# A hybrid encoder trunk: values of mixer C on 128 columns, squares of mixer A in PSUM, another order of the first transposes

## The chip, the cores and the metric

The kernel runs on one core of a Trainium2 chip. The metric is the time of one execution in device microseconds (us). The engines: PE (TensorE, products and transposes, writes PSUM), ACT (ScalarE), DVE (VectorE), POOL (GpSimd) and SP (here only a queue that issues DMAs). PSUM has eight banks of 128 partitions x 512 fp32 numbers.

## What is computed

256 tokens x 1024 channels in float32 go through two layers:

```
h = RMSNorm(x);  q,k,v of four mixers and four gates = split(h @ W_in)      # W_in: 1024 x 12544
A: differential attention, 4 heads of 128:  o = RMSNorm((softmax(q0 k0) - lam softmax(q1 k1)) v)
B: grouped-query attention, 8 heads       D: 2-D neighbourhood attention, 8 heads
C: dilated attention, 8 heads of 64: three groups of keys, (window, dilation) = (128,1), (512,4), (2048,16);
   the groups' outputs are combined by their softmax denominators
x += (sum_i sigmoid(gate_i) * (o_i @ P_i)) @ W_out
x += (silu(a) * b) @ W_down,   [a|b] = DWConv3(RMSNorm(x) @ W_up)           # 1024 x 5632, 2816 x 1024
```

For mixer C with 256 tokens, one softmax over the keys of all three groups gives the combination. A query sees up to 256 keys of group 0, and of groups 1 and 2 only keys of its own residue class. The kernel orders the tokens so that the first and the last 64 partitions of a tile of 128 queries belong to two classes with 64 keys each.

## The kernel before

**Weights.** The work is a list of jobs, 56 for the mixers of a layer and then W_out, W_up and W_down. A job is one load of 1 MB of weights (tile `w`, three buffers, on SP's queue, three jobs ahead), two splits of it and its products. A split (`split`) makes a high part on ACT (line 281) and the rest on DVE (line 282). A product of fp32 accuracy is three matmuls of such parts (`mm3`, lines 334 to 336): high by high, high by rest, rest by high. A block of the first projection (512 columns, 256 tokens) takes two jobs of 24 matmuls each and two PSUM banks of the tag `mm`, which has four; the other tags are `s` (one bank, scores), `tp` (two, transposes), `o` (one, products with values). Blocks come in the order of a string, `... gD1 vC0 qC0 qC2 bD1 kC2 vC1 vC2 gB0 ...`: q, k, v of a mixer and group, g a gate, b a branch product.

**Behind a block.** `qk_vec` normalises and rotates a block of q or k: squares on ACT into the tile `sq` (line 468), rotation on DVE (lines 479 and 480, which read the `mm` bank), a reduction of `sq` (line 482), rsqrt on POOL. `sq` has one buffer, which `sumsq` (the norms) and mixer A's `finish` take as well. A block of values is copied by ACT (lines 811, 817).

**Mixers.** A unit is one step of a mixer for 128 queries: `score` (scores, maximum, exponential), 1.25 jobs later `transp`, 2 jobs after the scores `pv`, the product with the values into `o`. `finish` divides by the denominators when the last unit of a tile is done. C has 8 units (heads) for each of 2 tiles, 0.8 jobs apart; A has 4 units for each tile.

**The order.** The program is traced job by job: after each quarter of a job's matmuls the functions hung there (`at`) are traced. From this a planner that simulates the engines fixes, when the kernel is built, the order of instructions on every engine and which instruction gets a buffer; earlier traced ones go first when they are ready. `behind(i)` keeps what is traced in it behind instruction `i` on `i`'s engine. On the chip every engine runs its list in order and waits at semaphores.

**The start** (`first_norm`). x comes by SP's and ACT's queues, the first weights in parts. PE runs products on zeros, spreads the row of gains over 128 partitions (line 1174), and transposes the normed x (line 420) in four sets (tile 0 or 1, half 0 or 1 of the channels), each evacuated by ACT (line 434) and DVE (line 437) into `hTh` and `hTl`. The first job's matmuls start on set (0, 0).

Of the kernel before, what the change touches and what calls it, by code (L numbers as in the profile page):

```python
# [10 lines left out]
F32 = mybir.dt.float32  # L11
F32R = mybir.dt.float32r
AF = mybir.ActivationFunctionType
ALU = mybir.AluOpType
AX = mybir.AxisListType

DM = 1024
# [9 lines left out]
MA, MB, MC, MD = range(4)  # L27
# [59 lines left out]
class Trunk:  # L87
# [324 lines left out]
            scaled(i)  # L412
        return xn

    def norm_tr(self, t, xn, by_token=False, halves=(0, 1)):

        for i in halves:
            p = self.ps("mm")
            for k in range(4):
                self.last_tr = self.nc.tensor.transpose(p[:, k * 128:(k + 1) * 128], xn[:, i * 512 + k * 128:i * 512 + (k + 1) * 128], self.ident).ins  # L420
            hl = [a[:, i * 4:i * 4 + 4, :] for a in (self.hTh, self.hTl)]
            if not by_token:
                last = self.evac_split([(four(p), *(half(a, t) for a in hl))])
                continue
            pv = p.rearrange("p (k u c r) -> p u k c r", k=4, u=2, c=16)
            tv = [a.rearrange("p k (r c u) -> p u k c r", r=4, c=16) for a in hl]
            last = self.evac_split([(pv[:, u], tv[0][:, 2 * t + u], tv[1][:, 2 * t + u]) for u in range(2)])
        return last
# [193 lines left out]
    def pv(self, u):  # L622
        nc = self.nc
        if u["m"] == MA and u["k"] % 2 == 0:
            return
        m, t, st, pt = u["m"], u["t"], u["st"], u["pt"]
        o = st.setdefault("o", {})
        if t not in o:
            o[t] = self.ps("o")
        o = o[t]  # L630
        v = st["v"]
        blk = lambda i: pt[:, i * 128:(i + 1) * 128]
        if m == MC:
            h = u["h"]
            s = slice(h * 64, (h + 1) * 64)
            for i in range(2):
                nc.tensor.matmul(o[:, s], blk(i), v[0][:, i, s], start=i == 0, stop=False)  # L637
            for b in range(2):
                nc.tensor.matmul(o[64 * b:64 * b + 64, s], blk(2)[:, 64 * b:64 * b + 64], v[1 + b][:, t, s], start=False, stop=True)
        elif m == MD:  # L640
            for i in range(4):
                h = 2 * i + u["k"]
                hs = slice(h * 64, (h + 1) * 64)
                for s in range(2):
                    nc.tensor.matmul(o[64 * s:64 * s + 64, hs], blk(i)[:, 64 * s:64 * s + 64], v[1 + t][:, s, hs], start=True, stop=True)
        elif m == MA:
            for c in range(2):
                h = u["k"] - 1 + c
                s = slice(h * 128, (h + 1) * 128)
                for i in range(2):  # L650
                    nc.tensor.matmul(o[:, s], blk(2 * c + i), v[0][:, i, s], start=i == 0, stop=i == 1)
        else:

            g, par = u["k"] // 2, u["k"] % 2
            ph, pl = (a.rearrange("p (i k q) -> p k i q", i=2, k=2) for a in pt)
            for i in range(2):
                vh, vl = (v[:, j, i, g * 64:g * 64 + 64] for j in range(2))
                self.mm3(o[:64, par * 256:(par + 1) * 256], ph[:, i], pl[:, i], vh, vl, i == 0, i == 1, stationary_w=True)
            if par:
                self.o_over_q(st, o, slice(2 * g, 2 * g + 2), t * 128, 128)  # L660
                del st["o"][t]
            return
        if u["last"]:
            self.finish(u, o)

    def finish(self, u, o):

        nc = self.nc
        m, t, st = u["m"], u["t"], u["st"]
        sums = st["sums"][t]  # L670
        nh = 4 if m == MA else 8
        d = 512 // nh
        hv = lambda a: a.rearrange("p (h d) -> p h d", d=d)
        if "osb" not in st:
            st["osb"] = self.t4([128, 2, 512])
        osb = st["osb"]
        r = self.small("rcp", 8)
        if m == MA:

            nc.vector.reciprocal(r[:, :4], sums.rearrange("p (h c) -> p h c", c=2)[:, :, 0])  # L680
            sq = self.sb(self.tp, "sq", [128, 2, 512], F32, bufs=1)[:, 0]
            nc.vector.tensor_tensor(hv(osb[:, t, :]), hv(o[:]), r[:, :4].unsqueeze(2).to_broadcast([128, 4, 128]), ALU.mult)
            nc.scalar.activation(sq, osb[:, t, :], AF.Square, scale=1.0 / math.sqrt(128.0))
            rr = self.small("rr", 4)
            nc.vector.tensor_reduce(rr, hv(sq[:]), AX.X, ALU.add)
            self.rsqrt_mean(rr[:, :4], rr[:, :4], 4)
            nc.vector.tensor_tensor(hv(osb[:, t, :]), hv(osb[:, t, :]), rr.unsqueeze(2).to_broadcast([128, 4, 128]), ALU.mult)
        else:
            nc.vector.reciprocal(r, sums)
            nc.vector.tensor_tensor(hv(osb[:, t, :]), hv(o[:]), r.unsqueeze(2).to_broadcast([128, 8, 64]), ALU.mult)  # L690
# [29 lines left out]
    def layer(self, l):  # L720
        nc = self.nc
# [75 lines left out]
        def vblock(m, col0, g=0):  # L797
# [4 lines left out]
            def ev():  # L802
                v = stt[m]["v"]
                if g == 0:
                    v.append(self.t4([128, 2, 512]))
                elif g == 1:
                    v.extend([self.t4([128, 2, 512]), self.t4([128, 2, 512])])
                for t in range(2):
                    o = cell["o"][t]
                    if g == 0:  # L810
                        nc.scalar.copy(v[0][:, t, :], o)
                        continue

                    for b in range(2):
                        r = slice(64 * b, 64 * b + 64)
                        w = r if g == 1 else slice(64 - 64 * b, 128 - 64 * b)
                        nc.scalar.copy(v[1 + b][w, t, :], o[r])

            def windows():

# [100 lines left out]
        for what in ORDER.split():  # L921
            kind, i, c = what[0], "ABCD".index(what[1]), int(what[2:] or 0)
            if what == "kB":
                bkv()
            elif kind in "qk":
                k = int(kind == "k")
                col0 = ((AQ, BQ, CQ, DQ), (AK, None, CK, DK))[k][i] + c * 512
                first = slot[0] == 0
# [211 lines left out]
    def first_norm(self):  # L1140

        nc, d = self.nc, self.d
        zero = self.sb(self.wp, "hi", [128, 1024], F32R, bufs=5)
        nc.vector.memset(zero[:].bitcast(F32), 0.0)
        warm = self.small("warm", 1, 1)
        nc.scalar.activation(warm, self.mhalf[:, :1], AF.Exp)
        job = self.jobs[0]
        job["w"] = self.sb(self.wp, "w", [128, 2048], F32, bufs=3)
        (dst, src), = job["src"](job["w"][:])
        part = lambda k, n: (dst[:, k:k + n], bass.AP(src.tensor, src.offset + k * 128 * N_IN, [src.ap[0], (src.ap[1][0], n), src.ap[2]]))  # L1150
        xrows = lambda u: (self.x[64 * (u % 2):64 * (u % 2) + 64, u // 2, :], self.rows("x", u, 0, DM))
        row = self.t4([1, DM])

        nc.sync.dma_start(*xrows(0))
        nc.scalar.dma_start(*xrows(1))
        nc.scalar.dma_start(*part(0, 1))
        nc.sync.dma_start(row, self.dram("norm1_g", 0, [[DM, 1], [1, DM]]))
        nc.sync.dma_start(*part(1, 1))
        nc.sync.dma_start(*part(2, 2))
        for u in (2, 3):  # L1160
# [4 lines left out]
        p = self.ps("s")  # L1165
        ones = self.small("ones", 128, 1)[:1]
        nc.gpsimd.memset(ones, 1.0)
        for i in range(10):
            last = nc.tensor.matmul(p, zero[:, :128], zero[:, :512], start=True, stop=True).ins

        g = [self.ps("tp") for i in range(2)]
        with self.behind((last,)):
            for i in range(2):
                nc.tensor.matmul(g[i], ones, row[:, i * 512:(i + 1) * 512], start=True, stop=True)

        def norm(t):
            ss = self.small("ss", 4)
            for i in range(2):
                self.sumsq(t, slice(i * 512, (i + 1) * 512), ss, i, vector=(t, i) == (0, 1))
            return self.norm_vec(t, g, ss, 2, lazy=True)  # L1180


        xn = [norm(0)]
# [1 line left out]
        with self.behind((self.last_xn,)):  # L1185
            self.split(0)
        with self.behind((self.last_split,)):
            last = self.norm_tr(0, xn[0][0], halves=(0,))
        with self.behind(last):
            self.split(1)  # L1190
            xn.append(norm(1))
            xn[1][1](0)

        def step(t, i, then):
            with self.behind((self.last_mm, self.last_split)):
                last = self.norm_tr(t, xn[t][0], halves=(i,))
            with self.behind(last):
                then()

        def first():  # L1200
            xn[0][1](1)
            self.split(2)

        def second():
            xn[1][1](1)
            self.split(3)

        def third():
            self.split(4)
            self.split(5)  # L1210

        self.at(0, 1, lambda: step(1, 0, first))
        self.at(0, 3, lambda: step(0, 1, second))
        self.at(1, 1, lambda: step(1, 1, third))
        self.at(1, 3, lambda: self.split(6))

def trunk_kernel(tc, d):
    with ExitStack() as ctx:
# [29 lines left out]
```

## Time and profile before

| | |
|---|---|
| three timed runs | 1246.92, 1249.25, 1251.32 us; median 1249.25 |
| profiled execution | 1249.13 us, span 1247.3 us, mean granted TensorE clock 0.993 |
| busy: PE, DVE, ACT, POOL | 1223.9, 901.3, 716.8, 134.4 us |

The span runs from the first instruction to the last; the execution's own time is a little longer. "Busy" counts the time in which an engine computes. PE's matmuls overlap in the pipeline, so a matmul's duration is longer than the distance to the next one; where rates matter, the text takes differences of start times.

### The profile page before, as it was taken

The page shows a single profiled execution, that of the slowest core. Times are in us where ns is not written, and L with a number is a line of the kernel's source. Part 1 is how long each engine was busy: PE and PEld are TensorE (multiplying, and loading weights), DVE is VectorE, ACT ScalarE, POOL GpSimd, SP SyncE. Part 2 cuts the span into 40 slices and gives each one's busy share as a digit, 9 for nine tenths or more (in the row PEclk, how much of TensorE's full clock was granted, in tenths as well). Part 3 has the DMA queues.
Part 4 walks back from the last instruction along what each step waited for, and adds up shares of the span by engine and source line. Part 5 has one row for each costly group of instructions (what it writes and reads, how often), then busy time and mean ns, then how long its engine had stood idle before and what let it go on. Part 6 is the DMA issues. An engine that isn't in the chain of part 4 may idle for free.

```text
span 1247.3 us, 18889 instructions
## 1 busy us (share of the span) xinstructions
PE 1223.9 (98%) x7394; PEld 1049.6 (84%) x7394; DVE 901.3 (72%) x1445; ACT 716.8 (57%) x1197; POOL 134.4 (11%) x88
## 2 busy tenths in 40 slices
PE   8999999989999999999999999999899999999998
PEld 5878888877888889998878888888688888999986
DVE  5997787874455679887478978869555456888853
ACT  4556767536444467665355766655455443777641
POOL 0332130320000000000023212203200000000000
PEclk8999999989999999999999999999999999999999
DMA  8757345444346646565544754374434353666551
GB/s 257 231 168 237 106 165 170 147 156 142 129 154 168 202 136 201 194 202 199 201 163 147 215 186 136 114 225 138 166 135 156 116 167 122 203 204 200 183 194 66
DMA packets 127671, 212.09 MB, mean 170 GB/s; under 512 B 9085, under 2 KB 56797, under 8 KB 127582
## 3 DMA queue, kind: packets, MB, share of 16 engines
q1 hardware_dynamic: 125758, 205.64, 50.3%
q0 software_dynamic: 1280, 4.20, 1.6%
q8 instruction: 58, 0.95, 0.3%
q10 hardware_dynamic: 544, 1.05, 0.3%
q14 instruction: 31, 0.25, 0.1%
HBM read 203.53 MB, written 1.05 MB: 164 GB/s over the span
## 4 chain that ended last, share of the span: by engine, by line
PE 95%; DMA 2%; ACT 1%; DVE 1%; issue 0%; ACTq 0%; SPq 0%
PE mm L334 18%; PE mm L336 18%; PE mm L335 18%; PE mm L332 6%; PE mm L331 6%; PE mm L330 6%; PE tp L613 2%; DMA w<-in_w_in_dram 2%; PE tp L334 2%; PE tp L335 2%; PE tp L336 2%; PE tp L493 1%; PE o L637 1%; PE s L532 1%; PE o L334 1%; PE o L335 1%
## 5 line engine op out<-in xcount | busy, mean ns | idle before, releaser
L282 DVE TENSOR_TENSOR lo<-w,hi 128x1024 fp32r<-128x1024 f32 x376 | 456.1, 1221 | 209.0 <-ACT hi L281 207.3
L281 ACT CAST hi<-w 128x1024 fp32r<-128x1024 f32 x376 | 392.4, 1052 | 298.6 <-PE mm L336 184.6
L334 PE MATMUL mm<-hi,hTh 128*128 128x512 f32 (+1 forms) x796 | 314.2, 396 | 11.5 <-DVE qn L480 7.6
L335 PE MATMUL mm<-lo,hTh 128*128 128x512 f32 (+1 forms) x796 | 313.3, 394 | 0.8 <-DVE lo L282 0.8
L336 PE MATMUL mm<-hi,hTl 128*128 128x512 f32 (+1 forms) x796 | 313.3, 395 | 0.0
L330 PE MATMUL mm<-hTh,hi 128*128 128x256 f32 x704 | 193.9, 276 | 1.2 <-ACT hTh L434 1.2
L332 PE MATMUL mm<-hTl,hi 128*128 128x256 f32 x704 | 194.1, 276 | 0.9 <-DVE hTl L437 0.9
L331 PE MATMUL mm<-hTh,lo 128*128 128x256 f32 x704 | 194.1, 276 | 0.0
L334 PEld LDWEIGHTS mm<-hi,hTh 128*128 128x128 f32 x796 | 151.0, 190 | 43.1 <-issue 8.7
L336 PEld LDWEIGHTS mm<-hi,hTl 128*128 128x128 f32 x796 | 150.6, 189 | 30.9 <-DVE hTl L437 1.7
L335 PEld LDWEIGHTS mm<-lo,hTh 128*128 128x128 f32 x796 | 150.8, 190 | 30.4 <-DVE lo L282 1.4
L330 PEld LDWEIGHTS mm<-hTh,hi 128*128 128x128 f32 x704 | 131.9, 188 | 1.7 <-ACT hTh L434 1.7
L332 PEld LDWEIGHTS mm<-hTl,hi 128*128 128x128 f32 x704 | 132.0, 188 | 1.3 <-DVE hTl L437 1.3
L331 PEld LDWEIGHTS mm<-hTh,lo 128*128 128x128 f32 x704 | 132.2, 188 | 0.0
L160 POOL TENSOR_TENSOR sm_qr<-sm_qr,mhalf 128x16 f32<-128x16 f32 (+1 forms) x24 | 81.1, 3380 | 2.0
L334 PE MATMUL mm<-hi,t 128*128 128x512 f32 (+1 forms) x192 | 74.6, 389 | 0.0
L335 PE MATMUL mm<-lo,t 128*128 128x512 f32 (+1 forms) x192 | 73.6, 383 | 0.0
L336 PE MATMUL mm<-hi,t 128*128 128x512 f32 (+1 forms) x192 | 73.0, 384 | 0.0
L1054 ACT ACTIVATE e<-mm,cwT 128x256 f32<-128x256 f32 x88 | 47.0, 560 | 27.8 <-PE mm L332 25.4
L402 POOL TENSOR_TENSOR sm_nr<-sm_nr,mhalf 128x1 f32<-128x1 f32 x8 | 4.4, 550 | 526.7 <-DVE sm_nr L399 517.9
L159 POOL TENSOR_SCALAR sm_qr<-sm_qr 128x16 f32<-128x16 f32 (+1 forms) x24 | 30.6, 1274 | 238.9 <-DVE sm_qr L482 238.7
L1055 DVE SCALAR_TENSOR_TENSOR e<-mm,cwT,e 128x255 f32<-128x255 f32 x88 | 39.6, 478 | 12.0 <-ACT e L1054 12.0
(177 smaller groups left out, 1670.0 us busy)
## 6 DMA issues: line engine op xcount, KB each, us to landing
w<-in_w_in_dram SPq DMA_DIRECT2D x97, 1024.0 KB, 5.1
w<-in_w_up_dram SPq DMA_DIRECT2D x44, 1024.0 KB, 5.1
w<-in_w_down_dram SPq DMA_DIRECT2D x22, 1024.0 KB, 4.9
w<-in_w_branch_dram SPq DMA_DIRECT2D x16, 1024.0 KB, 4.9
w<-in_w_out_dram SPq DMA_DIRECT2D x8, 1024.0 KB, 5.7
t<-t POOLq DMA_DIRECT2D x16, 256.0 KB, 5.6
t<-t SPq DMA_DIRECT2D x32, 64.0 KB, 3.1
t<-in_rpb_dram SPq DMA_DIRECT2D x32, 62.5 KB, 5.2
```

The source lines that it names most:

```text
L159: nc.gpsimd.tensor_scalar(dst, ss, EPS, None, op0=ALU.add)
L160: nc.gpsimd.tensor_tensor(dst, dst, mh, ALU.pow)
L281: self.nc.scalar.copy(hi, w)
L282: self.last_split = self.nc.vector.tensor_tensor(lo, w, hi[:].bitcast(F32), ALU.subtract).ins
L330: mm(out, wh, xh, start=first, stop=False)
L331: mm(out, wl, xh, start=False, stop=False)
L332: mm(out, wh, xl, start=False, stop=last)
L334: mm(out, xh, wh, start=first, stop=False)
L335: mm(out, xh, wl, start=False, stop=False)
L336: self.last_mm = mm(out, xl, wh, start=False, stop=last).ins
L1054: nc.scalar.activation(y[:, b:b + 256], o[:, b:b + 256], AF.Identity, scale=cw(1, z), bias=cw(3, z))
L1055: nc.vector.scalar_tensor_tensor(y[:, b + 1:b + 256], o[:, b:b + 255], cw(0, z), y[:, b + 1:b + 256], op0=ALU.mult, op1=ALU.add)
```

## The change

In C's `pv` the product with the values of group 0 repeats the 64 columns of a head, and groups 1 and 2 of both classes are one product, whose 128 columns are the two classes. Of each query row the half of its own class counts; `finish` takes it from there, after heads 0 to 3 and after heads 4 to 7 of a tile. The value tiles of groups 1 and 2 are laid out by query tile and class instead. A's `finish` writes its squares over its product in PSUM. At the start the row of gains goes by POOL's queue, its spreading comes after four of the products on zeros, the sets of transposes are evacuated from the banks `o` and `s`, and their places change: sets (1, 0) and (0, 1) after the first half of job 0, set (1, 1) after its third quarter.

```diff
-    def norm_tr(self, t, xn, by_token=False, halves=(0, 1)):
+    def norm_tr(self, t, xn, by_token=False, halves=(0, 1), tag="mm"):
-            p = self.ps("mm")
+            p = self.ps(tag)
...
         if m == MC:
+            oh = o[:, h % 4 * 128:h % 4 * 128 + 128]
             for i in range(2):
-                nc.tensor.matmul(o[:, s], blk(i), v[0][:, i, s], start=i == 0, stop=False)
-            for b in range(2):
-                nc.tensor.matmul(o[64 * b:64 * b + 64, s], blk(2)[:, 64 * b:64 * b + 64], v[1 + b][:, t, s], start=False, stop=True)
+                nc.tensor.matmul(oh, blk(i), v[0][:, i, s].unsqueeze(1).to_broadcast([128, 2, 64]), start=i == 0, stop=False)
+            nc.tensor.matmul(oh, blk(2), v[1 + t][:, :, s], start=False, stop=True)
+            if h % 4 == 3:
+                self.finish(u, o)
+                del st["o"][t]
+            return
...
         if m == MA:
-            sq = self.sb(self.tp, "sq", [128, 2, 512], F32, bufs=1)[:, 0]
-            nc.scalar.activation(sq, osb[:, t, :], AF.Square, scale=1.0 / math.sqrt(128.0))
+            nc.scalar.activation(o, osb[:, t, :], AF.Square, scale=1.0 / math.sqrt(128.0))
-            nc.vector.tensor_reduce(rr, hv(sq[:]), AX.X, ALU.add)
+            nc.vector.tensor_reduce(rr, hv(o[:]), AX.X, ALU.add)
+        elif m == MC:
+            h0 = u["h"] - 3
+            nc.vector.reciprocal(r[:, :4], sums[:, h0:h0 + 4])
+            for b in range(2):
+                w = slice(64 * b, 64 * b + 64)
+                nc.vector.tensor_tensor(hv(osb[w, t, h0 * 64:h0 * 64 + 256]), o[w].rearrange("p (h b d) -> p h b d", h=4, b=2)[:, :, b, :],
+                                        r[w, :4].unsqueeze(2).to_broadcast([64, 4, 64]), ALU.mult)
...
-                        nc.scalar.copy(v[1 + b][w, t, :], o[r])
+                        nc.scalar.copy(v[1 + t][w, b, :], o[r])
...
+        row = self.t4([1, DM])
+        nc.gpsimd.dma_start(row, self.dram("norm1_g", 0, [[DM, 1], [1, DM]]))
-        nc.sync.dma_start(row, self.dram("norm1_g", 0, [[DM, 1], [1, DM]]))
...
-        for i in range(10):
-            last = nc.tensor.matmul(p, zero[:, :128], zero[:, :512], start=True, stop=True).ins
-        with self.behind((last,)):
-            for i in range(2):
-                nc.tensor.matmul(g[i], ones, row[:, i * 512:(i + 1) * 512], start=True, stop=True)
+        last = None
+        for i in range(12):
+            with self.behind(last):
+                if i in (4, 5):
+                    last = nc.tensor.matmul(g[i - 4], ones, row[:, (i - 4) * 512:(i - 3) * 512], start=True, stop=True)
+                else:
+                    last = nc.tensor.matmul(p, zero[:, :128], zero[:, :512], start=True, stop=True)
+                last = (last.ins,)
...
-                self.sumsq(t, slice(i * 512, (i + 1) * 512), ss, i, vector=(t, i) == (0, 1))
+                self.sumsq(t, slice(i * 512, (i + 1) * 512), ss, i, vector=i == 1)
...
-            last = self.norm_tr(0, xn[0][0], halves=(0,))
+            last = self.norm_tr(0, xn[0][0], halves=(0,), tag="o")
         with self.behind(last):
             self.split(1)
+            xn[0][1](1)
             xn.append(norm(1))
-            xn[1][1](0)
+            for i in range(2):
+                xn[1][1](i)
...
-        self.at(0, 1, lambda: step(1, 0, first))
-        self.at(0, 3, lambda: step(0, 1, second))
-        self.at(1, 1, lambda: step(1, 1, third))
+        def second():
+            with self.behind((self.last_mm, self.last_xn)):
+                last = self.norm_tr(1, xn[1][0], halves=(0,), tag="s")
+            with self.behind((self.last_tr, *last)):
+                last = self.norm_tr(0, xn[0][0], halves=(1,), tag="o")
+            with self.behind(last):
+                self.split(2)
+        def third():
+            with self.behind((self.last_mm, self.last_split)):
+                last = self.norm_tr(1, xn[1][0], halves=(1,), tag="s")
+            with self.behind(last):
+                for i in range(3, 6):
+                    self.split(i)
+        self.at(0, 1, second)
+        self.at(0, 2, third)
```

## Rows read from the trace of the kernel before

**Rows 1.** The page, part 1: busy us (share of the span) and instructions.
```profile
PE 1223.9 (98%) x7394; PEld 1049.6 (84%) x7394; DVE 901.3 (72%) x1445; ACT 716.8 (57%) x1197; POOL 134.4 (11%) x88
```
**Rows 2.** Groups by line and shape: busy us, mean ns, idle before, releasers.
```profile
L334 PE MATMUL mm<-hi,hTh 128*128 128x512 f32 x764 | 305.4, 401 | 11.5 <-DVE qn L480 7.6 <-ACT hTh L434 2.9 <-ACT t L817 0.9
```
**Rows 3.** Stretches: length, busy us of PE, PEld, DVE, ACT, POOL; PE's clock, DMA.
```profile
255.00:268.00 13.00, 13.00 (x69) 10.94 (x67) 9.13 (x11) 5.60 (x7) 0.00 (x0) 1.00 0.59 195
271.60:278.40 6.80, 6.15 (x15) 4.83 (x16) 4.63 (x7) 0.00 (x0) 3.27 (x3) 0.50 0.00 0
...
290.00:392.00 102.00, 102.00 (x643) 83.72 (x642) 51.84 (x78) 52.34 (x89) 0.00 (x0) 1.00 0.41 136
...
886.00:889.40 3.40, 3.40 (x10) 2.62 (x9) 2.87 (x4) 0.00 (x0) 1.49 (x2) 0.50 0.00 0
```
**Rows 4.** Timeline of PE, kC2's end and vC2's start: start us, us, instruction.
```profile
254.34 0.39 PE L336 MATMUL mm<-hi,hTl 128*128 128x512 f32 x1
254.57 0.62 PE L334 MATMUL mm<-hi,hTh 128*128 128x512 f32 x2
...
272.25 0.77 PE L334 MATMUL mm<-hi,hTh 128*128 128x512 f32 x1 [3.79 <-DVE qn L480]
```
**Rows 5.** Timelines of ACT and DVE in the same stretch, layer 0.
```profile
268.02 0.63 ACT L683 ACTIVATE sq<-t 128x512 f32<-128x512 f32 x1
...
269.49 1.09 ACT L468 ACTIVATE sq<-mm 128x512 f32<-128x512 f32 x2
...
268.69 0.69 DVE L685 TENSOR_REDUCE sm_rr<-sq 128x4 f32<-128x512 f32 x1 [0.89 <-ACT sq L683]
...
270.76 0.75 DVE L479 TENSOR_TENSOR t<-mm,tab 128x256 f32<-128x256 f32 x2
271.43 0.68 DVE L480 TENSOR_TENSOR qn<-mm,tab 128x512 f32<-128x512 f32 x1
```
**Rows 6.** Timeline of PE: one unit of C's values, one of A's.
```profile
310.97 0.66 PE L637 MATMUL o<-t,pt 128*128 128x64 f32 x4
...
311.82 0.55 PE L613 MATMUL tp<-ident,e 128*128 128x128 f32 x3
...
231.96 1.05 PE L651 MATMUL o<-t,pt 128*128 128x128 f32 x8
232.77 0.48 PE L335 MATMUL mm<-lo,hTh 128*128 128x512 f32 x1
233.08 0.39 PE L336 MATMUL mm<-hi,hTl 128*128 128x512 f32 x1
```
**Rows 7.** DVE: the group nearest to the new finish; timeline of an old finish.
```profile
L437 DVE TENSOR_TENSOR t<-o,t 64x256 fp32r<-64x256 f32 x16 | 6.6, 415 | 3.8 <-ACT t L434 3.6
...
390.85 0.69 DVE L690 TENSOR_TENSOR t<-o,sm_rcp 128x512 f32<-128x512 f32 x1 [0.59 <-PE o L639]
```
**Rows 8.** Timeline of PE in the start.
```profile
1.97 4.12 PE L1169 MATMUL s<-hi 128*128 128x512 f32 x10 [1.97 <-DVE hi L1144]
6.11 1.95 PE L1174 MATMUL tp<-t,sm_ones 1*128 1x512 f32 x4
...
13.13 1.91 PE L357 MATMUL mm<-lo,hTh 128*128 128x512 f32 x4
14.84 0.97 PE L420 MATMUL mm<-ident,t 128*128 128x128 f32 x4
16.49 0.50 PE L334 MATMUL mm<-hi,hTh 128*128 128x512 f32 x1 [0.68 <-ACT hTh L434]
...
29.69 0.39 PE L334 MATMUL mm<-hi,hTh 128*128 128x256 f32 x2
```
**Rows 9.** Timeline of DVE in the start: the scaling of tile 1.
```profile
13.25 0.75 DVE L407 SCALAR_TENSOR_TENSOR t<-x,sm_nr,tp 128x512 f32<-128x512 f32 x1 [0.67 <-POOL sm_nr L402]
```
**Rows 10.** The page, part 6: DMA issues, count, KB each, us to landing.
```profile
t<-t POOLq DMA_DIRECT2D x16, 256.0 KB, 5.6
t<-t SPq DMA_DIRECT2D x32, 64.0 KB, 3.1
```

More of the change, by code (lines that the diff above doesn't have):

```diff
@@ L1151, in first_norm @@
         xrows = lambda u: (self.x[64 * (u % 2):64 * (u % 2) + 64, u // 2, :], self.rows("x", u, 0, DM))
-        row = self.t4([1, DM])
         nc.sync.dma_start(*xrows(0))
@@ L1187, in first_norm @@
         with self.behind((self.last_split,)):
-            last = self.norm_tr(0, xn[0][0], halves=(0,))
+            last = self.norm_tr(0, xn[0][0], halves=(0,), tag="o")
         with self.behind(last):
             self.split(1)
+            xn[0][1](1)
             xn.append(norm(1))
-            xn[1][1](0)
-        def step(t, i, then):
+            for i in range(2):
[8 more added lines that the diff above has]
+        def third():
             with self.behind((self.last_mm, self.last_split)):
-                last = self.norm_tr(t, xn[t][0], halves=(i,))
+                last = self.norm_tr(1, xn[1][0], halves=(1,), tag="s")
             with self.behind(last):
[L1198 to L1210, printed above, removed]
-        self.at(0, 1, lambda: step(1, 0, first))
-        self.at(0, 3, lambda: step(0, 1, second))
-        self.at(1, 1, lambda: step(1, 1, third))
+                for i in range(3, 6):
+                    self.split(i)
+        self.at(0, 1, second)
+        self.at(0, 2, third)
         self.at(1, 3, lambda: self.split(6))
+        self.first_xn = self.last_xn
 def trunk_kernel(tc, d):
```

## The prediction

> **What bounds the kernel now.** I read the page first: the share of each engine, and the shape of the span. PE is busy for 1223.9 of 1247.3 us [rows 1], so the kernel is bound by TensorE nearly everywhere, and the chain of waits runs along PE's products. That leaves two ways to be faster: less work on PE, or fewer of the 23.4 us in which it stands still. So the second view is the list of groups, where PE's idle time stands beside what ended it. Of the large products the group of line 334 carries most of it: 7.6 us ended by line 480 (twice 3.8), 2.9 us by line 434 in the first transposes, 0.9 us by line 817 [rows 2]. Third, the stretches around these stalls: after each of the two long ones PE's clock is granted at one half, 1.2 GHz in place of 2.4, for 6.8 us in layer 0 and 3.4 us in layer 1 [rows 3]. A stall here costs its own length and then slow products. Fourth, the timeline of PE, ACT and DVE at the places that the diff touches.
>
> The profiled execution took 1249.13 us, 1.83 more than its span; the three timed runs have their median at 1249.25, so what is taken from the profile holds for the median too.
>
> **Part 1: A's squares in PSUM.** The reader should look at 254 to 272 us. The product of block kC2 issues its last matmul at 254.34 [rows 4]. Its first reader on ACT, the square of line 468, starts at 269.49, 15 us later [rows 5], though ACT was busy for only 5.60 of the 13 us from 255 to 268 [rows 3]. Line 468 writes the tile `sq`, of which there is one buffer. Mixer A's second tile asks for the same tile earlier in program order, writes it at 268.02 (line 683) and has it read until 268.69 + 0.69 = 269.38 (line 685). The square of kC2 follows 0.11 us after that. So kC2's two `mm` banks stay full until line 480 has read them at 271.43 to 272.11, PE needs one of them for block vC2, and waits 3.79 us, until 272.25 [rows 4]. The copies of line 817 (block vC1) wait in ACT's order behind kC2's transposes and give the 0.9 us.
>
> With A's square written to the bank `o`, which A holds anyway, nothing of this chain is left before kC2's square: it can run at about 255, and its reads by lines 479 and 480 (0.75 + 0.68 for each of two banks, so 2.9 us of DVE [rows 5]) have 13 us, of which DVE was busy for 9.13 [rows 3], so 3.9 us idle. I count the two stalls, 7.6, and the 0.9. The slow stretches go with them: PE was busy for 6.15 us of the one and 3.40 of the other [rows 3], at half speed, so up to 3.1 + 1.7 = 4.8; I take 4.5, because a fill at the start of a run of products isn't doubled. Sum of part 1: 7.6 + 0.9 + 4.5 = **13.0 us**. Square and reduction themselves stay as they are: a reduction of 512 columns out of `sq` takes 0.69 [rows 5]. `o` is held for about 2 us more (square, wait, reduction), and its next product is several jobs away. Late next: kC2's chain through DVE, which has slack, then the weight splits. Bounds: 0, if it wasn't `sq` that held line 468, and 13.3.
>
> **Part 2: C's product with the values.** Each of 32 units (8 heads, 2 tiles, 2 layers) now issues eight passes: four of 64 columns on the full array (line 637, fp32 takes two passes for each product), four on half of its columns (line 639). At 310.97 they hold PE for 0.85 us until the next transposes [rows 6]. The new unit has six passes of 128 x 128 on 128 columns. Their nearest rows are A's (line 651): eight in 232.77 - 231.96 = 0.81, and the product behind them 0.31 in place of 0.23, so 0.89 for eight, 0.111 each; six are 0.67. Difference 0.85 - 0.67 = 0.18, times 32 = **5.9 us**. PE is busy for 102.00 of 102 us in this stage [rows 3], so all of it should show. Bounds: nothing, if the repeated operand slowed a pass to 0.142 (six of them are 0.85), and 8 if the passes came at 0.10 as the eight do without the product behind them (0.81 / 8).
>
> Here the Trainium skill speaks against the change. "TensorE: Matmul & The Clock Gate", section "Back-to-back issue gap", gives the gap of single matmuls as N/2.4 + 2.5 ns; by that 8 x 29 = 233 ns become 6 x 56 = 335 ns (an estimate from that page), 3.3 us slower over 32 units instead of 5.9 faster. The rows disagree: eight passes with 64 columns take 0.85, 0.106 each, and passes with 128 columns 0.111, so the columns up to 128 cost next to nothing here. The same page, section "LDWEIGHTS", gives a weight load of 128 columns 107 ns, which is what the trace shows as the distance.
>
> Off PE, each half tile is finished on its own: per tile two short reciprocals and four products on 64 partitions x 256, of which the nearest row has 0.415, against one reciprocal and 0.69 now [rows 7]. That adds 4 x 0.415 - 0.69 = 1.0 us of DVE and a reciprocal, four times, in a stage where DVE is busy for half of the time [rows 3]: nothing. But it adds a wait: the fifth head's product needs `o`, and behind it on PE stands everything else. Units are 0.8 of a job apart, 0.8 x 24 products x 0.23 = 4.4 us, and the finish takes about 1.2 (2 x 0.415, a reciprocal and the releases); the old finish started right behind its product (DVE had been idle for 0.59 us and was released by it [rows 7]). So nothing again; if that cover is gone, see the last rival. The copies into the value tiles (line 817) are as many and as large.
>
> **Part 3: the start.** PE runs 10 products on zeros from 1.97, the four passes that spread the gain from 6.11 to 8.06, and right behind them the first transposes; the transposes of tile 1 at 14.84, then 36 products of 512 columns from 16.49 to 29.69 with two more sets of transposes between them [rows 8]. Those 36 take 36 x 0.23 = 8.3 (254.57 - 254.34 [rows 4]), so 4.9 of the 13.2 us are transposes and waits for their evacuation, 2.9 of it in front of line 334 [rows 2]. In the new order the second and third set (tile 1 half 0, tile 0 half 1) run back to back into `s` and `o`, the evacuation of the one beside the transposes of the other; the fourth set goes between two runs of products, and its results are needed 18 products later. Left are one set on PE (0.5), a wait for the low half of hT (0.2) and fills (0.2): 9.2 instead of 13.2, **4.0 us** less, if 16.49 stays.
>
> What sets 16.49 is the transposes at 14.84: PE comes there from twelve products at half clock (0.43 each, [rows 8]), and the scaled tile 1 that they need is ready at 13.25 + 0.75 = 14.00 [rows 9]. The change puts a scaling (0.75) and a sum of squares for DVE (about as long) ahead of that, in place of a sum on ACT (about as long again): up to 14.8. So that is no loss while PE is as late. The gain's spreading moves in front of six of the zero products, and its row comes by POOL's queue. It must be there after four products, 1.97 + 4 x 0.43 + 0.2 = 3.9 us. The nearest rows for a DMA issued at about 1.0: 3.1 us to landing on SP's queue, 5.6 on POOL's (both for larger tiles) [rows 10], so 4.1 to 6.6. In the worst case PE pauses 2.7 us, the four passes at twice their 0.43 and six products at half clock end at 6.6 + 3.4 + 2.6 = 12.6 instead of 8.1, and the slip of 4.5 eats the 4.0. In the best the clock stays up into the first products and PE is early, but then the scaled tile 1 decides, for a further 0.5 to 1.5. "DMA: Bandwidth & Descriptors" of the Trainium skill, section "Anatomy of one DMA", fits a POOL DMA with 2.0 us and the bytes; by it (an estimate) the row lands near 3.5 and nothing slips. I take **3.0 us**, with -0.5 and 5.5 as bounds.
>
> SP loses one issue of 0.7 us ahead of the weights; the first products wait for the norm, not for them, so nothing.
>
> **Sum.** 13.0 + 5.9 + 3.0 = 21.9; 1249.1 - 21.9 = **1227 us**.
>
> **Rivals.**
> (a) A's tile wasn't the cause, or the stall comes back: if line 468 was held by the order that was planned for ACT, or kC2's chain now queues behind the weight splits on DVE, 5 to 13 us of part 1 remain: 1232 to 1240. For it: 2.9 us of new work in 3.9 us of idle time is not much room [rows 3]. Against it: the 0.11 us between the end of line 685 and line 468, the same stall in both layers, and that ACT idled before it.
> (b) The start gives nothing: the row lands late or the clock stays at half for longer. 1227 + 3 = 1230, and 1231.5 with the worst of its bounds.
> (c) A pass costs in proportion to its columns: six of 128 are 768 columns where eight of 64 were 512, so 0.85 us become 1.28, and 32 x 0.43 = 13.6 are lost instead of 5.9 won: 1227 + 19.5 = 1246.5, no change that can be told. Against it stand both rows, of 64 and of 128 columns. It is the direction of the page's rule on the issue gap, in its strongest form.
> (d) Slower: the wait for `o` in the middle of a tile. If the finish of heads 0 to 3 were late on DVE as kC2's reads were, PE would stand four times (two tiles, two layers) for 3.8 us beyond the 4.4, and lose about 3.1 to the clock each time: 4 x 6.9 = 27.6, 1227 + 27.6 = 1255. From 5.5 us per place it beats the 21.9 gained. For it: DVE runs its queue in order, and the output tile is now taken four units earlier. Against it: DVE is half idle there, and the old finish started at once.
>
> **How the numbers follow.** Forecast 0.60, 1222 to 1231 alone; (a) 0.18; (b) 0.11; (c) 0.03; (d) 0.04; 0.04 for a rearrangement elsewhere that I don't see. A difference of 0.3%, 3.7 us, is about what a measurement of this kernel can tell from none. (c) lies within it, (d) and a quarter of the last case are slower, the rest is faster by more: faster 0.91, within 0.3% 0.04, slower 0.05. The range for 8 in 10 runs from 1220 (start and passes at their best: 1227 - 2.5 - 2.1 and a little for other stalls) to 1237, which takes in (b), (c) and most of (a).
>
> **What would show it.** Part 1: line 468 for kC2 starts near 255, no idle time of line 334 ended by line 480, clock 1.00 from 250 to 300 and from 860 to 910. Part 2: six passes per unit in 0.67 us, no 64-column rows left at that line. Part 3: the products of the first two jobs end near 25.7 instead of 29.7; the pause before the gain's passes tells when its row landed. I am wrong if line 468 still waits with `sq` free, if a pass on the repeated operand takes clearly more than 0.11, or if the fifth head's product waits for DVE.

## The result, and the profile after

The kernel after takes 1233.65 us (median of four runs, 1232.88 to 1234.93), the kernel before 1249.42 in the same rounds: a ratio of 0.9876 [0.9856, 0.9896] (brackets hold 95% intervals), 15.8 us less. The forecast was 1227, so 6 of the 22 us that it counted did not come. The profiled execution took 1232.88 us, its span is 1231.1. The busy times of the engines (page, part 1), which answer to [rows 1]:

```profile
PE 1215.5 (99%) x7330; PEld 1045.9 (85%) x7330; DVE 905.4 (74%) x1463; ACT 716.1 (58%) x1195; POOL 134.5 (11%) x89
```

PE is busy for 8.4 us less and the span is 16.2 us shorter, so PE's idle time fell from 23.4 to 15.6 us. The group of line 334 had 11.5 us of idle time in [rows 2]. In the page of the kernel after:

```profile
L334 PE MATMUL mm<-hi,hTh 128*128 128x512 f32 (+1 forms) x796 | 312.3, 394 | 0.6 <-ACT hTh L434 0.5
```

Line 480 no longer ends any idle time of it. The stretches of [rows 3] again (the length and the busy times of PE, its weight loads, DVE, ACT and POOL, then PE's clock, the DMA share and GB/s):

```profile
255.00:268.00 13.00, 13.00 (x66) 10.89 (x66) 9.83 (x15) 6.26 (x8) 7.50 (x2) 1.00 0.63 226
271.60:278.40 6.80, 6.80 (x37) 5.36 (x36) 4.00 (x6) 5.68 (x10) 1.27 (x2) 1.00 0.49 165
290.00:392.00 102.00, 102.00 (x602) 85.09 (x601) 55.75 (x85) 50.14 (x81) 0.00 (x0) 1.00 0.47 149
886.00:889.40 3.40, 3.40 (x17) 2.85 (x18) 1.79 (x3) 3.17 (x7) 0.00 (x0) 1.00 0.93 303
```

The two stretches at a clock of 0.50 are at 1.00 now. Why shows in the timelines of ACT and DVE, to be read against [rows 5]:

```profile
255.01 1.29 ACT L468 ACTIVATE sq<-mm 128x512 f32<-128x512 f32 x2 [1.72 <-PE mm L336]
256.46 0.67 DVE L480 TENSOR_TENSOR qn<-mm,tab 128x512 f32<-128x512 f32 x1
257.72 0.67 DVE L480 TENSOR_TENSOR qn<-mm,tab 128x512 f32<-128x512 f32 x1
...
270.22 0.60 ACT L688 ACTIVATE o<-t 128x512 f32<-128x512 f32 x1
271.38 0.69 DVE L690 TENSOR_REDUCE sm_rr<-o 128x4 f32<-128x512 f32 x1
```

The square of block kC2 starts at 255.01 and not at 269.49; what it waits for is its own product. Both banks have been read at 258.4, before block vC2 asks for one. A's square (line 688 now) comes 15 us behind it and holds nobody.

The first product of the same index stands in both traces at nearly the same time from 30 to 250 us. Behind the first stall of before it is 5.6 to 5.9 us earlier, at the end of mixer C in layer 0 8.4, behind the second stall 13.3, at the end 15.9. So the gain came from the two stalls and from C, and the start gave nothing (at 30 us the kernel after is 0.2 us behind). The start in PE's timeline, to be read against [rows 8], and the issue of the row of gains on POOL:

```profile
1.98 2.08 PE L1188 MATMUL s<-hi 128*128 128x512 f32 x4 [1.98 <-DVE hi L1156]
6.74 3.75 PE L1186 MATMUL tp<-t,sm_ones 1*128 1x512 f32 x4 [2.69 <-DMA t<-in_norm_g_dram]
10.42 2.93 PE L1188 MATMUL s<-hi 128*128 128x512 f32 x6
13.14 0.73 PE L420 MATMUL o<-ident,t 128*128 128x128 f32 x4
14.54 0.72 PE L357 MATMUL mm<-hi,hTh 128*128 128x512 f32 x2 [0.68 <-ACT hTh L434]
...
19.31 0.63 PE L420 MATMUL s<-ident,t 128*128 128x128 f32 x4 [0.90 <-DVE t L407]
...
20.61 0.50 PE L334 MATMUL mm<-hi,hTh 128*128 128x512 f32 x1 [0.24 <-ACT hTh L434]
...
29.93 0.28 PE L335 MATMUL mm<-lo,hTh 128*128 128x256 f32 x1
...
1.32 0.73 POOL L1160 DMA_DIRECT2D t<-in_norm_g_dram  x1 [0.35 <-issue]
```

PE stands for 2.69 us until the row of gains has come, and six products on zeros follow its spreading. The first product begins at 14.54 (9.55 before), the 36 products at 20.61 (16.49), and the third job at 29.93 (29.69).

### The profile page after: what moved, and what is told of

It reads as the page before. It is cut to its first block, busy times and chain, and to the rows that moved or that the text cites. A ratio compares the mean times of both kernels' runs of the same rounds, so it can differ in the third digit from the quotient of the medians.

```text
span 1231.1 us, 18778 instructions
## 1 busy us (share of the span) xinstructions
PE 1215.5 (99%) x7330; PEld 1045.9 (85%) x7330; DVE 905.4 (74%) x1463; ACT 716.1 (58%) x1195; POOL 134.5 (11%) x89
## 4 chain that ended last, share of the span: by engine, by line
PE 97%; DVE 1%; ACT 0%; DMA 0%; issue 0%; POOL 0%; DVEq 0%; POOLq 0%
PE mm L336 18%; PE mm L335 18%; PE mm L334 18%; PE mm L332 7%; PE mm L330 6%; PE mm L331 6%; PE tp L613 2%; PE tp L334 2%; PE tp L336 2%; PE tp L335 2%; PE tp L493 2%; PE o L639 1%; PE s L532 1%; PE s L554 1%; PE o L336 1%; PE o L334 1%
## 5 line engine op out<-in xcount | busy, mean ns | idle before, releaser
L160 POOL TENSOR_TENSOR sm_qr<-sm_qr,mhalf 128x16 f32<-128x16 f32 (+1 forms) x24 | 76.5, 3189 | 2.0
L159 POOL TENSOR_SCALAR sm_qr<-sm_qr 128x16 f32<-128x16 f32 (+1 forms) x24 | 34.8, 1448 | 307.8 <-DVE sm_qr L482 307.6
```

The costliest lines, as they stand in the source:

```text
L159: nc.gpsimd.tensor_scalar(dst, ss, EPS, None, op0=ALU.add)
L160: nc.gpsimd.tensor_tensor(dst, dst, mh, ALU.pow)
```

## The experiments

They were run in three sets; the kernel before stood at 1249.18, 1249.08 and 1249.27 us in them.

**One part at a time.** First A's squares alone, on the kernel before:

```diff
-            sq = self.sb(self.tp, "sq", [128, 2, 512], F32, bufs=1)[:, 0]
...
-            nc.scalar.activation(sq, osb[:, t, :], AF.Square, scale=1.0 / math.sqrt(128.0))
+            nc.scalar.activation(o, osb[:, t, :], AF.Square, scale=1.0 / math.sqrt(128.0))
...
-            nc.vector.tensor_reduce(rr, hv(sq[:]), AX.X, ALU.add)
+            nc.vector.tensor_reduce(rr, hv(o[:]), AX.X, ALU.add)
```

> The kernel before with one edit: mixer A's squares go to PSUM. Theory (the single buffer held kC2's square back): line 468 for kC2 at about 255, both stalls of 3.8 us and the slow clock behind them gone, 13 us less: 1236 from 1249.4. Rival (the order on ACT held it, the other edits freed it): 1249. A difference of 10 or less would mean that something takes the stall's place.

Measured: 1237.85 us, ratio 0.9909 [0.9882, 0.9936], 11.3 less than 1249.18. Its group of line 334 keeps the start's waits and has lost line 480:

```profile
L334 PE MATMUL mm<-hi,hTh 128*128 128x512 f32 (+1 forms) x796 | 312.4, 393 | 3.0 <-ACT hTh L434 2.9
```

So the shared tile was the cause. Whether PSUM has a part in it, a second run tells: the squares stay in SBUF, in a tag with four buffers.

```diff
-            sq = self.sb(self.tp, "sq", [128, 2, 512], F32, bufs=1)[:, 0]
+            sq = self.sb(self.tp, "pt", [128, 512], F32, bufs=4)
```

> The kernel before, with A's squares left in SBUF but in a tile with four buffers of its own class (that of the softmax weights) instead of the single buffer of the group norms' squares. My theory, that the single shared buffer was the cause and PSUM has no part in it: both stalls before line 480 are gone and the time is 1236.5 to 1240 us, as with the squares in PSUM (1237.85). Rival, that the gain came from ScalarE writing to PSUM or from the changed planning around the new PSUM tile: the stalls stay, at 1247 to 1250 us.

Measured: 1239.12 us, ratio 0.9921 [0.9892, 0.9951]. ACT's timeline of this run has the square of kC2 at 254.83, and A's square in `pt` long behind it; no idle time of PE is ended by line 480:

```profile
254.83 1.29 ACT L468 ACTIVATE sq<-mm 128x512 f32<-128x512 f32 x2 [1.73 <-PE mm L336]
...
270.03 0.63 ACT L683 ACTIVATE pt<-t 128x512 f32<-128x512 f32 x1 [0.24 <-DVE t L682]
```

A free buffer in SBUF does it too. PSUM is only one place for it.

C's edit alone (the new `pv`, its `finish` and the layout of the values, as in the diff of the change):

```diff
...
-            for b in range(2):
-                nc.tensor.matmul(o[64 * b:64 * b + 64, s], blk(2)[:, 64 * b:64 * b + 64], v[1 + b][:, t, s], start=False, stop=True)
...
+            nc.tensor.matmul(oh, blk(2), v[1 + t][:, :, s], start=False, stop=True)
...
```

> The kernel before with mixer C's edit alone (product on 128 columns, finish by half tiles, layout of the values). Theory by the trace of the changed kernel: a unit with the transposes behind it takes 1.02 us instead of 1.16, 32 x 0.138 = 4.4 us less: 1245. The prediction's term: 5.9 less, 1243.5. Rival (a pass costs by its columns): 13.6 more, 1263; rival (the wait for the bank of the outputs in mid tile): slower than before, with PE idle in front of the fifth head's product.

Measured: 1245.72 us, ratio 0.9975 [0.9957, 0.9993], 3.5 less, between 0.9 and 5.4 by the interval; the spans of the profiled executions differ by 4.4 (1247.3 and 1242.9). Both stalls before line 480 are still in its trace. The new unit, in PE's timeline of the kernel after, first behind the scores on quarters of the array (line 554), then behind a product of 512 columns:

```profile
313.29 0.46 PE L554 MATMUL s<-t,t 64*64 64x64 f32 x8
313.68 0.71 PE L639 MATMUL o<-t,pt 128*128 128x128 f32 x4
314.23 0.39 PE L640 MATMUL o<-t,pt 128*128 128x128 f32 x2
314.45 0.49 PE L613 MATMUL tp<-ident,e 128*128 128x128 f32 x3
314.70 0.48 PE L334 MATMUL mm<-hi,hTh 128*128 128x512 f32 x1
...
299.15 0.61 PE L639 MATMUL o<-t,pt 128*128 128x128 f32 x4
299.59 0.39 PE L640 MATMUL o<-t,pt 128*128 128x128 f32 x2
299.82 0.49 PE L613 MATMUL tp<-ident,e 128*128 128x128 f32 x3
300.06 0.48 PE L334 MATMUL mm<-hi,t 128*128 128x512 f32 x1
```

Distances of starts are what to read. The unit takes 314.45 - 313.68 = 0.77 in the first place and 299.82 - 299.15 = 0.67 in the second. The two passes of line 640 take 0.22 to 0.23 in both, so 0.11 each; the 0.1 lies in the four before them, at the first pass behind the change from 64 x 64 quarters to the full array (the starts of single passes: 0.21 us from the first to the second there, 0.11 behind a product, 0.11 between the others in both places).

That columns are free up to 128 is tested by leaving half of them out, in the kernel after:

```diff
-                nc.tensor.matmul(oh, blk(i), v[0][:, i, s].unsqueeze(1).to_broadcast([128, 2, 64]), start=i == 0, stop=False)
-            nc.tensor.matmul(oh, blk(2), v[1 + t][:, :, s], start=False, stop=True)
+                nc.tensor.matmul(oh[:, :64], blk(i), v[0][:, i, s], start=i == 0, stop=False)
+            nc.tensor.matmul(oh[:, :64], blk(2), v[1 + t][:, 0, s], start=False, stop=True)
...
```

> The kernel after the change, with mixer C's six value passes on 64 columns instead of 128, still on the whole array; the second class's values are left out and its half of the output is written from the first class's. My theory, that a pass costs the same 0.11 us at 64 and at 128 columns: the unit stays at 0.65 to 0.77 us and the time at 1232 to 1235 us, as the kernel after. Rival, that passes cost by their columns: the unit falls by 6 x 0.05 us or so, over 32 units some 10 us, to 1223 to 1226 us.

Measured: 1233.05 us, ratio 0.9875 [0.985, 0.99]: as the kernel after. In its timeline of PE:

```profile
288.07 0.66 PE L639 MATMUL o<-t,pt 128*128 128x64 f32 x4
288.56 0.39 PE L640 MATMUL o<-t,pt 128*128 128x64 f32 x2
288.79 0.50 PE L613 MATMUL tp<-ident,e 128*128 128x128 f32 x3
```

Line 640's two passes take 0.23 with 64 columns as with 128, and the unit 0.72 against 0.77. By the starts of single passes, the 0.05 lies in the first pass of a unit alone (0.16 against 0.21 to the second, here behind the scores); the five behind it are 0.11 apart with 64 and with 128 columns. The span is 1.1 us shorter (1230.0), which is about 32 x 0.05 = 1.6. So the first pass of a unit costs by its columns and the others don't.

**The start.** Its edits alone, on the kernel before (the row on POOL's queue, the spreading behind four zero products, the transposes in their new places):

```diff
-        for i in range(10):
-            last = nc.tensor.matmul(p, zero[:, :128], zero[:, :512], start=True, stop=True).ins
+        for i in range(12):
+            with self.behind(last):
+                if i in (4, 5):
+                    last = nc.tensor.matmul(g[i - 4], ones, row[:, (i - 4) * 512:(i - 3) * 512], start=True, stop=True)
...
```

> The kernel before with the edits of the start alone. Theory (the row of gains lands at 6.7 us by POOL's queue, PE waits 2.7 us for it and the passes behind it run at half clock, which eats what the transposes win): within 1 us of before, the third job starting at 29.7 as before. The prediction's term: 3.0 less, 1246.4.

Measured: 1249.39 us, ratio 1.0 [0.9984, 1.0015]. PE waits 2.84 us for the row here too, and the third job starts at 30.05. Two edits were then taken back in the kernel after, the queue and the place of the spreading, leaving the transposes in their new places:

```diff
-        nc.gpsimd.dma_start(row, self.dram("norm1_g", 0, [[DM, 1], [1, DM]]))
...
+        nc.sync.dma_start(row, self.dram("norm1_g", 0, [[DM, 1], [1, DM]]))
...
-                if i in (4, 5):
+                if i in (10, 11):
...
```

> The changed kernel with the row of gains back on SP's queue behind the first half of x, and its spreading behind ten products on zeros as before; the transposes stay in their new order and banks. Theory: the new order of the transposes is worth about 4 us once the row doesn't delay PE: third job at 25.7 to 26 us, 1229.7. Rival (the scaling of tile 1, now later on DVE, decides): third job at 28 or later, less than 2 us better than the changed kernel's 1233.7.

Measured: 1229.4 us (1228.82 to 1230.03), ratio 0.984 [0.981, 0.987], the lowest so far. PE's timeline of this run:

```profile
1.98 4.63 PE L1188 MATMUL s<-hi 128*128 128x512 f32 x10 [1.98 <-DVE hi L1156]
6.54 2.35 PE L1186 MATMUL tp<-t,sm_ones 1*128 1x512 f32 x4
8.95 0.66 PE L420 MATMUL o<-ident,t 128*128 128x128 f32 x4
10.28 0.87 PE L357 MATMUL mm<-hi,hTh 128*128 128x512 f32 x2 [0.67 <-ACT hTh L434]
...
16.35 0.50 PE L334 MATMUL mm<-hi,hTh 128*128 128x512 f32 x1 [0.24 <-ACT hTh L434]
...
25.66 0.28 PE L335 MATMUL mm<-lo,hTh 128*128 128x256 f32 x1
```

No pause; the 36 products begin at 16.35, and the third job at 25.66, 4.3 us earlier than in the kernel after. Two runs tell the edits apart, each with one of the two edits of the last diff.

> The kernel after the change, with the gain's row back on SP's queue behind the first half of x, but its spreading still behind four zero products. The zero products end at about 4.1 us; the row, issued at 1.5 us, lands between 4.9 and 6.5 us (it was there at 6.54 in the run with ten zero products). My theory: the pause of TensorE comes from the order, not from the queue, so 1 to 2.4 us of pause stay, the clock rises late again, and the time is 1231 to 1233.5 us. Rival, that the queue alone is the cause: no pause, and 1229 to 1230 us.

Measured: 1233.72 us, ratio 0.9879 [0.9857, 0.9901], 0.2 above what was expected and no better than the kernel after:

```profile
6.21 3.75 PE L1186 MATMUL tp<-t,sm_ones 1*128 1x512 f32 x4 [2.16 <-DMA t<-in_norm_g_dram]
```

On SP's queue the row comes 0.5 us earlier, and PE still stands for 2.16 us; the 36 products begin at 20.12.

> The kernel after the change, with the gain's row left on POOL's queue, but its spreading put back behind ten zero products. My theory: the row lands at about 6.7 us as in the kernel after; the ten zero products last until about 6.5, so TensorE pauses for under 0.3 us, the first full product begins at about 10.3 us (14.54 in the kernel after) and the time is 1229 to 1230 us. Rival, that POOL's queue itself (its later rows, or the identity that is made later on POOL) delays the start: the time stays at 1232 to 1234 us.

Measured: 1231.15 us (1229.51 to 1235.14), ratio 0.9859 [0.9832, 0.9885]. PE doesn't wait for the row, and its 36 products begin at 16.34, as with SP's queue. So the early place of the spreading is what the start lost, and POOL's queue doesn't delay the start. But the median was 1.2 to 2.2 us above expectation, and by the starts of the same products its profile lost 2.5 us against the one with SP's queue around 1045, far from the start. The last set asks whether that is chance.

> The same kernel as the run gain_after_ten (row on SP's queue, spreading behind ten zero products), timed in more rounds beside its neighbour with the row on POOL's queue and the kernel after. My theory: 1229.4 us again, 4 us below the kernel after, and the same as its neighbour within 1 us, because the two start alike (16.35 and 16.34 us) and the neighbour's profile lost its 2.3 us behind the pauses at 1040 us, where its granted clock was 0.81 from 1034 to 1052. Rival, that the POOL queue costs about 2 us by itself: 1229.4 against 1231.

> The same kernel as the run pool_row_after_ten (row on POOL's queue, spreading behind ten zero products). My theory: within 1 us of ten_sp_again, 1229 to 1230.5 us, and a granted clock of 1.00 from 1034 to 1052 in a profile that is not disturbed there. Rival, that the queue costs about 2 us: 1231 us with a clock of 1.00 there.

> The kernel after itself, in the same rounds as the two versions with ten zero products: 1233.5 us, 4 us above both, if the early spreading is what the start lost.

Measured: 1229.15 us (1228.75 to 1229.75, ratio 0.9834 [0.9815, 0.9854]) with SP's queue, 1230.91 (1230.42 to 1231.5, ratio 0.9849 [0.983, 0.9869]) with POOL's, and 1236.83 (1232.94 to 1240.47, ratio 0.9894 [0.9869, 0.9918]) for the kernel after, where 1233.5 was expected. My expectation of "within 1 us" failed: the 1.8 us between the queues are there twice. The starts are again nearly alike: PE now waits 0.39 us for the row with SP's queue and 0.63 with POOL's, because the ten zero products took 4.0 to 4.1 us instead of 4.6, and the 36 products begin at 16.72 and 16.83. The stretch around the norm before W_up in layer 1, with columns as above, first with POOL's queue, then with SP's:

```profile
1034.00:1052.00 18.00, 15.85 (x121) 14.89 (x120) 13.75 (x23) 10.96 (x18) 0.55 (x1) 0.91 0.30 95
```

```profile
1034.00:1052.00 18.00, 15.64 (x131) 14.77 (x131) 13.68 (x24) 11.15 (x19) 0.55 (x1) 1.00 0.30 99
```

Both pause there alike (1.39 and 0.50 us for the norm and its first transposes, read off the timelines). Then the clock falls in the one and stays up in the other, and the slow products cost 1.2 us; in the first pair it was 0.81 against 1.00 and 2.5 us. Two POOL profiles have the fall, two SP profiles don't. It accounts for the profiled executions, but not for the medians: of the five runs with POOL's queue in the last set, two had a mean granted clock of 1.000 and took 1231.43 and 1231.5 us, while the three with 0.995 took 1230.42 to 1230.91; in the set before, one of four had 1.000 and took 1231.17. These speak for the rival, that the queue costs about 2 us by itself; by what path, when the starts are alike, no run shows, and it stays open. The fall doesn't belong to POOL's queue as such either: the kernel after has its pause 4 us later and no fall in its two profiles, and the run with A's squares in SBUF, whose row goes by SP's queue, has 0.96 in the same stretch. The kernel after moved by 3.2 us in its median between sets (three of its six runs in the last took 1239.21 to 1240.47, the others 1232.94 to 1234.45) while its two profiled spans are 1231.1 and 1231.2; its lowest run, 1232.88, is 4.1 above the lowest with ten zero products, 1228.75.

## Why the prediction was right, and where it was not

The time of 1233.65 lies in the stated range, but outside the forecast's own 1222 to 1231. By the time alone it would have been rival (a), 1232 to 1240, which did not occur; the range held because it was drawn to take in the rivals. What came is the cause of part 1 as argued, a smaller part 2 and no part 3.

**Part 1 (13.0 us).** Right in cause, place and nearly in size: 11.3 us by the medians of the part alone, 12.3 by its span (1247.3 - 1235.0). Of the span's difference 0.7 is there before 35 us, in the start, which this edit leaves alone; by the starts of the same products 6.4 come in layer 0 and 5.2 in layer 1, so 11.6. The waits of 7.6 and 0.9 are gone, and the slow products were sized right: behind the stalls 13 and 7 came 0.43 us apart instead of 0.23, which with the slow ones at their ends is about 4.4. The 1.3 us between this sum and 11.6 no run places. All its signs came: line 468 at 255, the clock at 1.00, and with the stalls the wait behind line 817. Rival (a) is out: DVE had 9.83 us of work in the 13 us where I feared for room, and the reads of kC2 were not late.

**Part 2 (5.9 us).** Right in direction, but it came a quarter lower, and by another path. The first failed step is the pair of rows: the 0.85 us of the old unit was taken behind the 64 x 64 scores, the 0.67 of the new one from A's rows, whose passes follow work on the full array. 16 of the 32 units come right behind the scores, and the 0.1 us of that change, which was in the 0.85, is in the new unit too (0.77). In the others 0.67 held, and the old unit was 0.75. A unit and the three transposes behind it took 1.156 us behind the scores before (0.854 + 0.302) and 1.018 after (0.771 + 0.247); behind a large product 1.050 and 0.912. Both fell by 0.138, not 0.18, which makes 32 x 0.138 = 4.4. The difference to the 3.5 of the medians is within their interval.

The second failed step is the price of the old passes, 0.106 each for eight alike. Two lines of the unit of [rows 6] show that they were not alike, line 639's four on half of the array's columns and the product behind the transposes:

```profile
311.56 0.34 PE L639 MATMUL o<-t,pt 128*64 128x64 f32 x4
312.12 0.48 PE L336 MATMUL mm<-hi,hTl 128*128 128x512 f32 x1
```

Line 637's four passes hold PE for 0.59 us (311.56 - 310.97), line 639's four for 0.26, the transposes for 0.30; in the kernel after the first four take 0.55, the last two 0.22, the transposes 0.25. By the starts of single passes, full-array passes behind the first follow each other in 0.11 us before and after; the last one ahead of line 639 took 0.21, and the first transpose behind line 639 took 0.17, where it takes 0.11 behind a full-array pass. So most of the gain is that the step to half of the columns and back is gone (0.09 + 0.06 a unit). The two passes fewer gave 0.04, because the four were cheap, and the first pass, now with 128 columns, costs 0.05 more.

Rival (c) is out by the 64-column run. It was the Trainium skill's rule in "TensorE: Matmul & The Clock Gate", section "Back-to-back issue gap", that spoke for it: by N/2.4 + 2.5 ns the six passes should cost 335 ns against 233 for eight narrower ones (an estimate from that page). The section itself calls this the gap of an isolated matmul, which at few columns counts too little because it leaves out the weight loads of a stream. The measured distance was 0.11 us with 64 and with 128 columns for all but the first pass of a unit, so for these fp32 passes the measurement decides against the formula.

**Part 2, off PE.** Hidden, as argued. The new finish takes 0.420 us for each product of 64 x 256, against 0.415 in [rows 7]. No pass of the fifth head waits for `o` in the trace, so rival (d) did not occur.

**Part 3 (3.0 us).** Wrong: rival (b), with 0.11, was the case. Nearly all of its worked worst case came true. It put the row's landing at 6.6 us and the pause at 2.7; they were about 6.7 and 2.69. It put the end of spreading and zero products at 12.6; it was 13.1. The slip at the first transposes was 13.14 - 8.22 = 4.9. The stretch from the first product to the 36 gave 0.9 of it back: it took 6.1 us from 14.54 to 20.61 and 6.9 from 9.55 to 16.49 before, where the products came 0.43 apart (granted clock 0.50 from 10.4 to 14.5); now they came down to 0.23 (clock 1.00), though PE waited 0.90 us for the scaled tile 1. So the 36 products began 4.1 later, which ate the 3.9 that the new order of the transposes gives (13.2 us from 16.49 to 29.69 before, 9.3 from 20.61 to 29.93). That order was sized right: 9.2 forecast, 9.3 in the kernel after and 25.66 - 16.35 = 9.3 with ten zero products. What failed was the choice between 4.1 and 6.6 for the landing: I weighed rows for SP's and POOL's queue and took 1 us off for the chance of a slip, where the POOL row alone spoke for a certain one. SP's queue would not have saved it (6.21 in the run with four zero products), and the page of before had a row for a load out of DRAM on SP's queue, nearer than the 3.1, that puts the landing at 6.2 or later for an issue at 1.0:

```profile
t<-in_rpb_dram SPq DMA_DIRECT2D x32, 62.5 KB, 5.2
```

The Trainium skill's "DMA: Bandwidth & Descriptors", section "Anatomy of one DMA", gave 2.0 us and the bytes; from the issue at 1.32 it was 5.4 us, so here the measurement decides.

So 13.0 + 5.9 + 3.0 became 11.3 + 3.5 + 0 by the parts alone, 14.8 against 15.8 for all three together (12.4 in the last set), which their intervals don't tell apart. 1.7 us of the miss are in part 1, 2.4 in part 2 and 3.0 in part 3.

## What to carry to other kernels

A tile with one buffer that two stages share ties them in the order in which the program asks for it: when an engine idles before an instruction whose input has long been there, look for who last held its output tile, and give one of the two any free buffer. Where a part's price has two ends, one of which eats the gain, take the nearest row as the price and move the wait behind work that is there anyway, as the ten zero products were here. A row for the cost of a pass is good only with the same neighbours ahead of it and behind it, and a mean over passes of several shapes is the price of none of them.

## What the runs showed of the hardware that was not expected

- The first passes on the full array behind passes on 64 x 64 quarters cost about 0.1 us more than behind a product of 512 columns: 314.23 - 313.68 = 0.55 against 299.59 - 299.15 = 0.44 for the four passes of line 639.
- fp32 passes of 128 rows on the full array come 0.11 us apart with 64 and with 128 columns; only the first pass of a unit is shorter with 64 (0.16 against 0.21 us behind the scores). Four passes on half of the array's columns held PE for 0.26 us, but the passes at the two ends of them took 0.09 and 0.06 longer.
- In the first microseconds the clock column can't be taken at its word. Two stretches of the run with SP's queue and ten zero products (columns as above):

```profile
4.00:6.00 2.00, 2.00 (x7) 1.50 (x5) 0.23 (x1) 0.29 (x1) 0.00 (x0) 1.00 1.01 273
12.00:13.00 1.00, 1.00 (x4) 0.78 (x3) 1.00 (x3) 0.00 (x0) 0.00 (x0) 0.50 1.06 373
```

  In the first, at a shown 1.00, the zero products of 512 columns come 0.46 us apart (4.63 for ten); in the second, at 0.50, the products come 0.43 apart; later ones at 1.00 come 0.23 apart. The spreading's four passes took 3.75 us behind a pause of 2.69, and behind ten products without a pause 2.35 in this run and 1.95 in the kernel before. What set them apart no run shows.
- Two kernels whose pauses at 1040 us are alike can differ in the clock granted behind them (0.91 and 1.00 over 18 us), which cost 1.2 us in the profiled execution. The 1.8 us between their medians are not explained by it: POOL's runs at a mean clock of 1.000 were no faster.
